# Hybrid SSD/attention layer on one core: transposed products as three 256-column matmuls per contraction tile, weights shifted by 64 bytes

## The chip, the cores and the metric

The kernel runs on one core of a Trainium2 chip. The metric is the device time of one execution in microseconds (us); lower is better. TensorE (PE) multiplies; its weight loads (PEld) are instructions of their own. ScalarE (ACT) and VectorE (DVE) do the elementwise work, GpSimd (POOL) a little of it, and SyncE (SP) issues most DMAs.

## The reference

One layer for 256 tokens of width 2048, all in float32:

```python
h = rmsnorm(x, g_mix) @ w_in                 # 2048 -> 5728 columns
z, xbc, dt, q, k, v, qi, ki, wi = _split(h, IN_SIZES)
xbc = jax.nn.silu(causal_dwconv(xbc, conv_w, conv_b))
...                                          # y_ssd: chunked SSD, gated by z, normalized
...                                          # y_att: attention over 64 keys chosen by the qi, ki, wi scores
x = x + jnp.concatenate([y_ssd, y_att], axis=-1) @ w_out      # 2048 -> 2048
u = rmsnorm(x, g_mlp) @ w_up                                  # 2048 -> 8192
return x + jnp.square(jax.nn.relu(u)) @ w_down                # 8192 -> 2048
```

The four weight matrices hold 207 MB less a little, and each is read from HBM once.

## The kernel before

**Split operands.** Every operand of a big product is split into two float32r parts, hi (the rounded value) and lo (the rest), and a product is the sum of three partial products: hi·hi, lo·hi and hi·lo. `operands` (L110) makes the parts of a weight block: SP loads `raw`, ACT casts it to `whi` (L122), DVE subtracts to get `wlo` (L123). `raw` has RB = 4 buffers, `whi` and `wlo` WB = 5 each. All this is emitted with a priority 600 instructions ahead of its place (HP); ACT and DVE are ordered by a scheduler that goes by such priorities, TensorE by the program's order alone (`manual_schedule`).

**Two kinds of product.** In `product` the tokens stand on the output's partitions: the activations are the stationary operand (the "weights" of TensorE) and the weight block streams as the moving operand, three matmuls of 512 columns (304 in the blocks m0 and m1) per token block and contraction tile, L141 to L143. In `product_t` the output's columns stand on partitions: 128-column slices of `whi` and `wlo` are the stationary operand, and the activations stream. The activations stand in `hx` or `x2x`, for each contraction tile `kt` as 512 columns, hi of the 256 tokens and then lo. L181 streams all 512 over the hi weights, into both halves of an accumulator bank (hi·hi in the first half, lo·hi in the second), L182 streams the first 256 over the lo weights into the second half. `total` adds the halves (L190, L191). One call of `product_t` makes 32 such pairs: four `operands` blocks of 1024 columns, eight slices each.

**Where `product_t` stands.** In the input projection for the blocks qi (4 calls) and xbc (6 calls), with `hx` streaming, and in the MLP for `w_up` (32 calls), with `x2x` streaming: 42 calls, 1344 pairs. The MLP runs up(0), up(1), down(0), up(2), down(1), up(3), down(2), down(3), where down is `product` on `w_down`. Between the big products the tasks of a list (SSD, attention, top-k choice) are advanced by `step`, a few instructions of PE at a time. The block m1, a `product` with 304 columns, follows the ten calls of the input projection; at that time DVE also does the convolution (L497) and the top-k choice (L469, L470).

**Addresses.** The tiles are allocated one behind the other in each partition, so their addresses follow from their sizes. In the built program `hx` (and `x2x`, in the same place) begins at byte 17632, the `whi` buffers at 87264 and every 4096 bytes on, the `wlo` buffers at 107744 and every 4096 on, `uh` and `ul` (the activations of down) at 129504 and further. All of these are 96 more than a multiple of 128. Two unused tiles, `gap0` (192 bytes, ahead of `hx`) and `gap1` (64 bytes, behind it), are part of that arrangement. In the blocks m0 and m1 alone, every second contraction tile streams from the second half of a block of 608 columns, 1216 bytes further on, which is 64 more than a multiple of 128, while its stationary operand stays where it was.

Of the kernel before, what the change touches and what calls it, by code (L numbers as in the profile page):

```python
# [10 lines left out]
F32R = mybir.dt.float32r  # L11
# [5 lines left out]
P = 128  # L17
D = 2048
T = 256
NB = T // P  # L20
KT = D // P
# [7 lines left out]
WARM = 9  # L29
WB = 5  # L30
RB = 4


Z0, XBC0, DT0, Q0, K0, V0, QI0, KI0, WI0, END = (
# [31 lines left out]
def hymba_kernel(ctx: ExitStack, tc: tile.TileContext, xn, xt, w_in, w_out, w_up, w_down, vcol, vrow, out):  # L66
    nc = tc.nc
    ctx.enter_context(tc.manual_schedule(engines={nc.tensor.engine}))
    keep = ctx.enter_context(tc.tile_pool(name="keep", bufs=1))
    wts = ctx.enter_context(tc.tile_pool(name="wts", bufs=1))  # L70
# [24 lines left out]
    def step():  # L95
        for t in list(tasks):
            if isinstance(t[1], int) and t[1] > 0:
                t[1] -= 1
            elif not isinstance(t[1], str) or t[1] in done:
                advance(t)  # L100
# [6 lines left out]
        return vc[:, VC[name] + i:VC[name] + i + 1]  # L107


    def operands(src, n, load=None):  # L110

        with tc.high_priority(offset=HP):
            raw = wts.tile([P, n], F32, name="raw", tag="raw", bufs=RB)
            hi = wts.tile([P, n], F32R, name="whi", tag="whi", bufs=WB)
            lo = wts.tile([P, n], F32R, name="wlo", tag="wlo", bufs=WB)
            step = n if load is None else n // 2
            for i in range(0, n, step):
                s = slice(i, i + step)
                nc.sync.dma_start(raw[:, s], src[:, s])
                if load is not None:  # L120
                    load()
                nc.scalar.copy(hi[:, s], raw[:, s])  # L122
                nc.vector.tensor_tensor(lo[:, s], raw[:, s], hi[:, s].bitcast(F32), op=OP.subtract)  # L123
        return hi, lo
# [4 lines left out]
    def accumulators():  # L129
        return [ps.tile([P, 512], F32, name="acc", tag="acc") for _ in range(2)]  # L130

    def product(src, n, left, load=None, tail=None):
# [16 lines left out]
        for kt in range(KT):  # L149
            if kt % 2 == 0:  # L150
                hi, lo = operands(src[kt // 2], 2 * n, load)
            w = slice(kt % 2 * n, kt % 2 * n + n)
            wh, wl = hi[:, w], lo[:, w]
            if kt < last:
                part(kt, acc[0][:, :n], 0, wh, wl)
                if tail is None:
                    part(kt, acc[1][:, :n], 1, wh, wl)
                else:
                    for i, (b, c) in enumerate(halves):
                        part(kt, acc[1 + i][:, c], b, wh[:, c], wl[:, c])  # L160
            else:
                kept.append((kt, wh, wl))
            step()
# [7 lines left out]
    def product_t(src, right):  # L171

        acc = accumulators()
        for i in range(4):
            hi, lo = operands(src[i], 1024)
            c = i % 2
            for k in range(8):
                kt = 8 * (i // 2) + k
                x = right(kt)
                s = slice(k * P, (k + 1) * P)  # L180
                nc.tensor.matmul(acc[c], hi[:, s], x, start=(kt == 0), stop=False)  # L181
                nc.tensor.matmul(acc[c][:, T:], lo[:, s], x[:, :T], start=False, stop=(kt == KT - 1))  # L182
                if k % 4 == 3:
                    step()
        return acc
# [53 lines left out]
    for name, cols in IN_BLOCKS:  # L239
        n = sum(b - a for a, b in cols)  # L240
# [8 lines left out]
    def in_pair(name, i):  # L249
        o = in_off[name][0] + i * 256 * D  # L250
        return product_t(w_in[o:o + 256 * D].rearrange("(h p c) -> h p c", h=4, p=P), lambda kt: hx[:, kt, :])
# [501 lines left out]
    def x2(kt):  # L753
        if kt >= KT - 4:
            need("res3")
        return box[0][:, kt, :]

    first = product_t(w_up[0], x2)
    while tasks:
        step()  # L760
# [11 lines left out]
    def up(q):  # L772
        uh = mlp.tile([P, KT, T], F32R, name="uh")
        ul = mlp.tile([P, KT, T], F32R, name="ul")
        for j in range(8):
            r = mlp.tile([P, 2, T], F32, name="r")
            total(r, first if q + j == 0 else product_t(w_up[8 * q + j], x2))
            nc.vector.scalar_tensor_tensor(r, r, 0.0, r, op0=OP.max, op1=OP.mult)
            s = slice(2 * j, 2 * j + 2)
            nc.scalar.copy(uh[:, s, :], r)  # L780
            nc.vector.tensor_tensor(ul[:, s, :], r, uh[:, s, :].bitcast(F32), op=OP.subtract)
        return uh, ul
# [72 lines left out]
```

## Time and profile before

| | |
|---|---|
| time before, median of 3 runs | 1114.1 us (1113.76 to 1115.49) |
| the profiled execution: its time | 1113.72 us |
| its span in the trace | 1111.7 us |
| PE busy | 1101.4 us, 99% of the span |
| PEld busy | 938.4 us, 84% |
| DVE busy | 692.5 us, 62% |
| ACT busy | 534.2 us, 48% |
| HBM read | 204.29 MB, 186 GB/s over the span with what is written |

The span is the time from the first to the last instruction in the trace. Matmuls are pipelined, and a row's own duration contains its latency; what a stream of them costs is read from the spacing of their starts in the timeline. Times in the trace are counted from the start of the span.

### The profile page before, as it was taken

Reading aid. Unit: us, or ns where it says so; the run is one execution under the profiler, and the core shown is the slowest. Engines: PE = TensorE matmul, PEld = TensorE weight load, DVE = VectorE, ACT = ScalarE, POOL = GpSimd, SP = SyncE. Lnnn points to the kernel's source line nnn. Section 1 sums busy time; section 2 is a strip of 40 time slices with the busy share of each in tenths; the row PEclk is TensorE's granted clock in tenths of the full one; section 3 lists DMA queues with packets and bytes.
Section 4 is the critical chain, followed back from the end, with each engine's and each line's share of the span. In section 5 each row is a group of like instructions: output and inputs, shape, how many; then the busy total and the mean of one; then the engine's idle time right before and its main releaser. Section 6 shows DMA issues by size and latency. Waiting matters only on the chain.

```text
span 1111.7 us, 14959 instructions
## 1 busy us (share of the span) xinstructions
PE 1101.4 (99%) x5686; PEld 938.4 (84%) x5686; DVE 692.5 (62%) x976; ACT 534.2 (48%) x749; POOL 41.5 (4%) x41
## 2 busy tenths in 40 slices
PE   9999998999999999999999999999999999999998
PEld 7888887888888888888888888888888888888887
DVE  6786989677765565656564455565555565555443
ACT  7755655556755444444444334444334444333341
POOL 0010131112000000000000000000000000000000
PEclk9999999999999999999999999999999999999999
DMA  9855435644376555556555665556666556666662
GB/s 309 276 191 186 155 106 167 197 152 133 118 261 187 176 187 187 184 182 188 188 189 190 193 196 183 188 188 191 193 195 193 181 186 190 196 194 194 209 212 73
DMA packets 63735, 207.36 MB, mean 187 GB/s; under 512 B 7216, under 2 KB 11568, under 8 KB 63664
## 3 DMA queue, kind: packets, MB, share of 16 engines
q1 hardware_dynamic: 63520, 206.36, 58.0%
q8 instruction: 45, 0.74, 0.3%
q14 instruction: 26, 0.21, 0.0%
q10 hardware_dynamic: 144, 0.05, 0.0%
HBM read 204.29 MB, written 2.10 MB: 186 GB/s over the span
## 4 chain that ended last, share of the span: by engine, by line
PE 95%; DVE 3%; issue 1%; DMA 0%; ACT 0%; POOL 0%; DVEq 0%; POOLq 0%; ACTq 0%
PE acc L181 27%; PE acc L141 17%; PE acc L143 16%; PE acc L142 16%; PE acc L182 14%; DVE wlo L123 1%; DVE bc L497 1%; PE ps_y L568 1%; DVE sc L461 1%; PE ps_sr L652 0%; PE ps_l L606 0%; PE ps_o L631 0%; DMA raw<-in_w_in 0%; PE ps_w L200 0%; PE ps_dec L559 0%
## 5 line engine op out<-in xcount | busy, mean ns | idle before, releaser
L123 DVE TENSOR_TENSOR wlo<-raw,whi 128x1024 fp32r<-128x1024 f32 (+3 forms) x400 | 467.0, 1170 | 382.9 <-ACT whi L122 380.0
L122 ACT CAST whi<-raw 128x1024 fp32r<-128x1024 f32 (+3 forms) x400 | 400.0, 1003 | 500.0 <-PE acc L142 247.0
L181 PE MATMUL acc<-x2x,whi 128*128 128x512 f32 x1024 | 362.2, 399 | 0.0
L182 PE MATMUL acc<-x2x,wlo 128*128 128x256 f32 x1024 | 287.6, 281 | 0.0
L181 PEld LDWEIGHTS acc<-x2x,whi 128*128 128x128 f32 x1024 | 192.4, 188 | 47.8
L142 PE MATMUL acc<-whi,ul 128*128 128x512 f32 (+1 forms) x512 | 197.6, 386 | 0.0
L141 PE MATMUL acc<-whi,uh 128*128 128x512 f32 (+1 forms) x512 | 197.6, 386 | 0.0
L143 PE MATMUL acc<-wlo,uh 128*128 128x512 f32 (+1 forms) x512 | 197.5, 386 | 0.0
L182 PEld LDWEIGHTS acc<-x2x,wlo 128*128 128x128 f32 x1024 | 193.4, 189 | 0.1
L181 PE MATMUL acc<-hx,whi 128*128 128x512 f32 x320 | 113.9, 398 | 0.0
L141 PEld LDWEIGHTS acc<-whi,uh 128*128 128x128 f32 x512 | 96.1, 188 | 19.6
L143 PEld LDWEIGHTS acc<-wlo,uh 128*128 128x128 f32 x512 | 96.1, 188 | 19.4
L142 PEld LDWEIGHTS acc<-whi,ul 128*128 128x128 f32 x512 | 96.2, 188 | 19.3
L182 PE MATMUL acc<-hx,wlo 128*128 128x256 f32 x320 | 89.7, 280 | 0.0
L143 PE MATMUL acc<-wlo,hx 128*128 128x512 f32 (+1 forms) x224 | 82.7, 369 | 3.3 <-DVE wlo L123 3.1
L141 PE MATMUL acc<-whi,hx 128*128 128x512 f32 (+1 forms) x224 | 85.4, 381 | 0.0
L142 PE MATMUL acc<-whi,hx 128*128 128x512 f32 (+1 forms) x224 | 82.1, 367 | 0.0
L181 PEld LDWEIGHTS acc<-hx,whi 128*128 128x128 f32 x320 | 60.2, 188 | 13.6
L182 PEld LDWEIGHTS acc<-hx,wlo 128*128 128x128 f32 x320 | 60.5, 189 | 0.0
L143 PEld LDWEIGHTS acc<-wlo,hx 128*128 128x128 f32 x224 | 42.3, 189 | 11.7 <-DVE wlo L123 5.2
L141 PEld LDWEIGHTS acc<-whi,hx 128*128 128x128 f32 x224 | 42.4, 189 | 6.9 <-issue 0.7
L142 PEld LDWEIGHTS acc<-whi,hx 128*128 128x128 f32 x224 | 42.4, 189 | 6.5 <-issue 0.7
(224 smaller groups left out, 828.9 us busy)
## 6 DMA issues: line engine op xcount, KB each, us to landing
raw<-in_w_up SPq DMA_DIRECT2D x128, 512.0 KB, 3.6
raw<-in_w_down SPq DMA_DIRECT2D x128, 512.0 KB, 4.2
raw<-in_w_in SPq DMA_DIRECT2D x72, 512.0 KB, 3.7
raw<-in_w_out SPq DMA_DIRECT2D x32, 512.0 KB, 3.6
raw<-in_w_in SPq DMA_DIRECT2D x16, 256.0 KB, 4.4
raw<-in_w_in SPq DMA_DIRECT2D x16, 152.0 KB, 5.3
raw<-in_w_in SPq DMA_DIRECT2D x8, 304.0 KB, 2.8
xT<-in_xt SPq DMA_DIRECT2D x16, 128.0 KB, 4.3
```

The costliest lines, as they stand in the source:

```text
L122: nc.scalar.copy(hi[:, s], raw[:, s])
L123: nc.vector.tensor_tensor(lo[:, s], raw[:, s], hi[:, s].bitcast(F32), op=OP.subtract)
L141: nc.tensor.matmul(out, ah[:, s], wh, start=(kt == 0), stop=False)
L142: nc.tensor.matmul(out, al[:, s], wh, start=False, stop=False)
L143: nc.tensor.matmul(out, ah[:, s], wl, start=False, stop=(kt == KT - 1))
L181: nc.tensor.matmul(acc[c], hi[:, s], x, start=(kt == 0), stop=False)
L182: nc.tensor.matmul(acc[c][:, T:], lo[:, s], x[:, :T], start=False, stop=(kt == KT - 1))
L461: nc.vector.scalar_tensor_tensor(sc[:, :nk], rl[:, i, :nk], wis[:, b, h:h + 1], neg[:, T - nk:] if first else sc[:, :nk], op0=OP.mult, op1 ...
L497: nc.vector.scalar_tensor_tensor(o[:, j, :], pad[:, j, k:k + T], vcp("conv_w", 12 * k + ct), o[:, j, :], op0=OP.mult, op1=OP.add)
L568: nc.tensor.matmul(pt[:, 64 * i:64 * i + 64], m[i // 4][:, i % 4, :], xdt[:, c, 64 * h:64 * h + 64], start=True, stop=True)
```

## The change

`operands` allocates one tile for both parts, of 2n columns and 64 spare ones, and takes hi and lo as slices of it that begin `shift` elements in. `product` uses shift 0, `product_t` 16 elements, 64 bytes. The L181 matmul of 512 columns becomes two of 256, and the order in a contraction tile is hi weights on hi activations, lo weights on hi activations, hi weights on lo activations. Each has a weight load of its own, so the hi slice is loaded twice.

```diff
+SPARE = 64
+SHIFT_T = 16
...
-    def operands(src, n, load=None):
+    def operands(src, n, load=None, shift=0):
...
-            hi = wts.tile([P, n], F32R, name="whi", tag="whi", bufs=WB)
-            lo = wts.tile([P, n], F32R, name="wlo", tag="wlo", bufs=WB)
+            both = wts.tile([P, 2 * n + SPARE], F32R, name="w2", tag="w2", bufs=WB)
+            hi, lo = both[:, shift:shift + n], both[:, shift + n:shift + 2 * n]
...
-            hi, lo = operands(src[i], 1024)
+            hi, lo = operands(src[i], 1024, shift=SHIFT_T)
...
-                nc.tensor.matmul(acc[c], hi[:, s], x, start=(kt == 0), stop=False)
-                nc.tensor.matmul(acc[c][:, T:], lo[:, s], x[:, :T], start=False, stop=(kt == KT - 1))
+                nc.tensor.matmul(acc[c][:, :T], hi[:, s], x[:, :T], start=(kt == 0), stop=False, skip_group_check=True)
+                nc.tensor.matmul(acc[c][:, T:], lo[:, s], x[:, :T], start=False, stop=False, skip_group_check=True)
+                nc.tensor.matmul(acc[c][:, T:], hi[:, s], x[:, T:], start=False, stop=(kt == KT - 1),
+                                 skip_group_check=True)
```

In the built program of the change the joint buffers begin at byte 87264 and every 8448 bytes on, so hi and lo stand 96 behind a multiple of 128 in `product`, as before, and 32 behind one in `product_t`; `hx` and `x2x` keep their place, and all tiles behind the buffers move by 1280 bytes.

On TensorE the place is the inside of `product_t` in the MLP. Before, with `whi` and `wlo` as the weights and `x2x` streaming:

```order
L181 MATMUL acc<-x2x,whi 128x512
L182 MATMUL acc<-x2x,wlo 128x256
L181 MATMUL acc<-x2x,whi 128x512
L182 MATMUL acc<-x2x,wlo 128x256
L181 MATMUL acc<-x2x,whi 128x512
L182 MATMUL acc<-x2x,wlo 128x256
```

Now, where `w_4162` is one joint buffer and lines are 3 to 5 higher:

```order
L184 MATMUL acc<-x2x,w_4162 128x256
L185 MATMUL acc<-x2x,w_4162 128x256
L186 MATMUL acc<-x2x,w_4162 128x256
L184 MATMUL acc<-x2x,w_4162 128x256
L185 MATMUL acc<-x2x,w_4162 128x256
L186 MATMUL acc<-x2x,w_4162 128x256
L184 MATMUL acc<-x2x,w_4162 128x256
L185 MATMUL acc<-x2x,w_4162 128x256
L186 MATMUL acc<-x2x,w_4162 128x256
```

A contraction tile has three rows in the place of two, and each row has 256 columns. The order around `product_t` is the same on TensorE.

The scheduler also orders DVE's queue anew around the end of the input projection. The place is that of the weight blocks of m1 (608 columns each): before, with `sc` the scores from which the top-k choice takes its maxima and `bc` the convolution's output,

```order
L123 TENSOR_TENSOR wlo<-raw,whi 128x608
L191 TENSOR_TENSOR xraw<-acc,xraw 128x256
L469 MAX m_2011<-sc_1689 128x8
L470 MATCH_REPLACE sc_1689<-m_2011,sc_1689 128x256
L123 TENSOR_TENSOR wlo<-raw,whi 128x608
L497 SCALAR_TENSOR_TENSOR bc<-pad,vc,bc 128x256 x3
L123 TENSOR_TENSOR wlo<-raw,whi 128x608
L497 SCALAR_TENSOR_TENSOR bc<-pad,vc,bc 128x256 x2
L123 TENSOR_TENSOR wlo<-raw,whi 128x608
```

and now

```order
L126 TENSOR_TENSOR w_2302<-raw,w_2302 128x608
L196 TENSOR_TENSOR xraw<-acc,xraw 128x256
L475 MATCH_REPLACE sc_1907<-m_2272,sc_1907 128x256
L474 MAX m_2292<-sc_1907 128x8
L126 TENSOR_TENSOR w_2322<-raw,w_2322 128x608
L502 SCALAR_TENSOR_TENSOR bc<-pad,vc,bc 128x256 x2
L126 TENSOR_TENSOR w_2342<-raw,w_2342 128x608
L502 SCALAR_TENSOR_TENSOR bc<-pad,vc,bc 128x256 x3
L126 TENSOR_TENSOR w_2374<-raw,w_2374 128x608
```

Between the last four of m1's subtractions stand the same kinds of instructions in nearly the same number; one convolution step stands one subtraction later, and the search and replace steps of the choice have traded places.

## Rows read from the trace of the kernel before

**Rows 1.** Page, busy time of the engines and the granted TensorE clock in 40 slices

```profile
PE 1101.4 (99%) x5686; PEld 938.4 (84%) x5686; DVE 692.5 (62%) x976; ACT 534.2 (48%) x749; POOL 41.5 (4%) x41
...
PEclk9999999999999999999999999999999999999999
```

**Rows 2.** Page, the chain that ended last, shares by engine and by line

```profile
PE 95%; DVE 3%; issue 1%; DMA 0%; ACT 0%; POOL 0%; DVEq 0%; POOLq 0%; ACTq 0%
PE acc L181 27%; PE acc L141 17%; PE acc L143 16%; PE acc L142 16%; PE acc L182 14%; DVE wlo L123 1%; DVE bc L497 1%; PE ps_y L568 1%; DVE sc L461 1%; PE ps_sr L652 0%; PE ps_l L606 0%; PE ps_o L631 0%; DMA raw<-in_w_in 0%; PE ps_w L200 0%; PE ps_dec L559 0%
```

**Rows 3.** Page, groups: busy us, mean ns of one, idle before and what ended it

```profile
L122 ACT CAST whi<-raw 128x1024 fp32r<-128x1024 f32 (+3 forms) x400 | 400.0, 1003 | 500.0 <-PE acc L142 247.0
L181 PE MATMUL acc<-x2x,whi 128*128 128x512 f32 x1024 | 362.2, 399 | 0.0
L182 PE MATMUL acc<-x2x,wlo 128*128 128x256 f32 x1024 | 287.6, 281 | 0.0
L181 PE MATMUL acc<-hx,whi 128*128 128x512 f32 x320 | 113.9, 398 | 0.0
```

**Rows 4.** Timeline of PE inside w_up: start us, duration us, instruction

```profile
699.89 0.40 PE L181 MATMUL acc<-x2x,whi 128*128 128x512 f32 x1
700.13 0.28 PE L182 MATMUL acc<-x2x,wlo 128*128 128x256 f32 x1
700.25 0.40 PE L181 MATMUL acc<-x2x,whi 128*128 128x512 f32 x1
...
700.95 0.40 PE L181 MATMUL acc<-x2x,whi 128*128 128x512 f32 x1
```

**Rows 5.** Windows (length; PE, PEld, DVE, ACT, POOL busy us): qi/xbc, m1, up(0, 1), up(2)

```profile
100.00:168.00 68.00, 68.00 (x416) 60.46 (x415) 58.83 (x112) 38.50 (x67) 14.45 (x13) 1.00 0.43 136
168.00:188.00 20.00, 16.30 (x109) 14.87 (x108) 19.55 (x40) 10.57 (x18) 4.08 (x3) 1.00 0.47 140
396.40:578.20 181.80, 181.80 (x1034) 157.87 (x1033) 113.05 (x147) 86.26 (x118) 0.00 (x0) 1.00 0.59 186
665.30:755.70 90.40, 90.40 (x513) 78.44 (x512) 54.21 (x63) 41.23 (x54) 0.00 (x0) 1.00 0.59 187
```

**Rows 6.** Waits of PE over the span: us in total, times, longest

```profile
PE acc L143 <- DVE wlo L123: 3.1, 3, 1.8
```

**Rows 7.** Timeline of PE inside down(0): only 512-column matmuls

```profile
600.00 0.39 PE L141 MATMUL acc<-whi,uh 128*128 128x512 f32 x1
...
600.68 0.39 PE L141 MATMUL acc<-whi,uh 128*128 128x512 f32 x1
```

**Rows 8.** Timeline of PE at the end of down(3): only 256-column matmuls

```profile
1105.90 0.28 PE L141 MATMUL acc<-whi,uh 128*128 128x256 f32 x1
1106.02 0.28 PE L142 MATMUL acc<-whi,ul 128*128 128x256 f32 x1
1106.14 0.28 PE L143 MATMUL acc<-wlo,uh 128*128 128x256 f32 x1
...
1107.34 0.28 PE L141 MATMUL acc_t<-whi,uh 128*128 128x256 f32 x1
```

**Rows 9.** Timeline of PE, plain float32 matmuls of 64 and 256 columns, merged to their end

```profile
220.56 1.61 PE L568 MATMUL ps_y<-room,mt 128*128 128x64 f32 x13
...
221.23 0.94 PE L568 MATMUL ps_y<-room,mt 128*128 128x64 f32 x7
...
239.21 1.46 PE L606 MATMUL ps_l<-room,qT 128*128 128x256 f32 x6
...
239.86 0.81 PE L606 MATMUL ps_l<-room,qT 128*128 128x256 f32 x3
```

**Rows 10.** Timeline of PE inside m1: first matmul of contraction tiles 0 to 4

```profile
168.10 0.30 PE L141 MATMUL acc<-whi,hx 128*128 128x304 f32 x1
...
168.93 0.30 PE L141 MATMUL acc<-whi,hx 128*128 128x304 f32 x1
...
169.76 0.30 PE L141 MATMUL acc<-whi,hx 128*128 128x304 f32 x1
...
170.59 0.30 PE L141 MATMUL acc<-whi,hx 128*128 128x304 f32 x1
...
171.43 0.30 PE L141 MATMUL acc<-whi,hx 128*128 128x304 f32 x1
```

## Prediction

> **What bounds the kernel now.** I read the page's busy times first: TensorE is busy 99% of the span, and its granted clock is full in every slice, that is 2.4 GHz [rows 1]. The chain of waits says the same from the other end: 95% of what ended last is TensorE, and 41% of it are the two lines that the change touches, L181 and L182 [rows 2]. So a nanosecond on each of their matmuls is a nanosecond on the kernel, but the groups can't give that price: one L181 is listed with 399 ns and one L182 with 281 [rows 3], and these overlap. The price is the spacing of starts. Inside w_up three pairs take from 699.89 to 700.95 us, 1060 ns, so a pair costs 353.3 ns [rows 4]. That the pair is repeated 1024 + 320 = 1344 times is in the groups' counts [rows 3]; 1344 x 353.3 ns = 475 us, which is the 41 to 43% of the chain. In the windows of up(0) to up(2) TensorE has no idle time at all, while DVE is busy for 60% and ACT for less than half [rows 5]: there nothing but TensorE's own stream sets the pace. The one wait of note is in m1, where TensorE waits 3.1 us for DVE's subtraction [rows 6], and DVE is busy for 19.55 of 20 us [rows 5].
>
> **What a matmul of each size costs.** Where 512-column matmuls follow one another, three take 600.00 to 600.68, 226.7 ns each [rows 7]. 512 columns at 2.4 GHz are 213.3 ns, so 13.3 ns are lost on each. Where only 256-column matmuls follow one another, each with a weight load of its own, twelve take 1105.90 to 1107.34: 120.0 ns each [rows 8], again 13.3 over their 106.7. The loss is one for each matmul, whatever its length. The mixed pair loses 33.3 over the 320 ns of its 768 columns, a little more than twice 13.3; the split of this is not to be seen.
>
> **The change, part by part.**
>
> *Three matmuls of 256.* The columns stay 768. By the row that is nearest, the 256-column stream [rows 8], a contraction tile costs 3 x 120.0 = 360.0 ns in the place of 353.3: +6.7 ns, x 1344 = **+9.0 us**, of which 6.8 in the MLP (1024) and 2.1 in qi and xbc (320). The third weight load is in the 120 ns: each matmul of that row loads its own. The bounds: below, if each of the three lost as little as the L182 of a pair seems to, 0.12 us from 700.13 to 700.25 at this row's resolution [rows 4], nothing would be lost or gained; at the very least a weight load needs some spacing, and the tightest stream of loads and matmuls in the trace, 64-column ones at full latency, has (221.23 - 220.56)/6 = 112 ns [rows 9]; 3 x 112 = 336 would be -17.3 ns, -23.3 us. Above, another loss of the same size, 13.3 ns per matmul, would be +62.7 us.
>
> The Trainium skill (TensorE: Matmul & The Clock Gate, Back-to-back issue gap) gives a warm matmul N/2.4 + 2.5 ns. By that the triple would cost one 2.5 ns more than the pair, an estimate of +3.4 us; the rows show a loss of 13.3, not 2.5, for float32r matmuls that each load weights, so the measurement decides, and the sign is the same.
>
> *64 bytes.* This is the part that the trace nearly lacks. Everywhere else stationary and moving operand begin at the same place modulo 128 bytes. The exception is m1: in its odd contraction tiles the weights begin 64 bytes further, modulo 128, than what streams, just as in the change. Tiles 0 and 2 (even) take 168.10 to 168.93 and 169.76 to 170.59, 0.83 us each for six matmuls; tiles 1 and 3 (odd) 0.83 and 0.84 [rows 10]. So 138.3 to 140 ns for 304 columns, 11.7 to 13.3 over their 126.7 in both positions. I take the shift at nothing. It has a doubt: six matmuls and then the other position, so the row does not show a long stream in the shifted one. Taking the low end of it, 11.7, the triple is 355.0, +1.7 ns, +2.3 us.
>
> What speaks for an effect is that the 13.3 ns are not the price of exchanging weights: plain float32 matmuls of 256 columns, a load each, are spaced (239.86 - 239.21)/3 = 217 ns [rows 9], about 3 over two passes of 106.7. They ask for their moving columns at half the pace. So the loss looks like two readers in each other's way, and that could depend on the address.
>
> The Trainium skill speaks against it (TensorE: Matmul & The Clock Gate, What happens when you issue a matmul): streaming and loading have independent read ports, and loading the next weights takes no read bandwidth from the running matmul. By that the shift is worth exactly nothing; no row here shows the ports themselves.
>
> *Joint buffers.* A cast into a joint buffer now has to wait until the last reader of either part is done, one matmul later at most (0.23 us). ACT is idle for 500 us ahead of its casts, 247 of them waiting for TensorE to free a buffer [rows 3], because it runs up to five blocks ahead; that lead covers it, and I cost it at nothing. In m1, where there is no lead, it could cost 8 blocks x 0.14 = 1.1 us.
>
> *DVE's new order.* The rows from the built programs show the same work between m1's last subtractions, a convolution step later by one. TensorE reaches m1 2.1 us later, for DVE partly time won: of the 3.1 us of waiting [rows 6] I give back one. The bound is 2.1 back or 2 more.
>
> *Sum*, against the profiled execution's own 1113.72 us: +6.8 + 2.1 - 1.0 = +7.9, 1121.6. The median of the runs is 0.4 us higher, so for the measurement **1122.0 us**, +0.7%. Its own range is 1116.4 (11.7 ns lost per matmul) to 1125 (all of the 9.0 and 2 us more waiting in m1).
>
> **The rivals.**
>
> 1. *Faster: the 64 bytes part the two readers.* Then the loss per matmul falls from 13.3 towards 5, the 112 ns of the tightest row [rows 9]: -23.3 us, 1090.8. Half of the loss gone (113.3 ns, 340 per tile) gives -17.9, 1096. It decides from 117.8 ns on: below that the triple is cheaper than the pair. For it: the float32 rows, whose loss is small though weights change as often. Against: the odd tiles of m1, which show nothing of it. The forecast of this case is 1093, and its range 1090 to 1111.
>
> 2. *No change.* The stream of three keeps the L182's 117 to 118 ns [rows 4] in place of the 120 of the pure stream, and 3 x 117.8 is the pair's 353.3. That gives 1114, and with what m1 does 1112 to 1116.
>
> 3. *Much slower: the shifted stream falls in a worse beat.* One half of the loss more on each matmul, 126.7 ns, is 380 per tile: +26.7 ns, +35.8 us, 1150. For it only that the mixed pair already loses more than its parts do; against it again m1.
>
> **How the numbers follow.** A difference of 0.2% (2.2 us) is about what measuring this kernel can tell from none. The forecast has 0.45, since its price comes from a stream of the same matmuls and the one shifted row agrees; the faster rival 0.39, because the shifted position in a long stream is nowhere in the trace and the loss that it could remove is as large as 13.3 x 3 per tile; no change 0.09; much slower 0.07. So faster 0.39, within 0.2% 0.09, slower 0.52. The range has to take in the faster rival: 1090 to 1125 leaves out the much slower case and a few hundredths below the tightest row, under 2 in 10; the forecast alone is 1116.4 to 1125.
>
> **What would show it.** In the timeline of w_up, three starts of L184 to L186 every 360 ns and 0.12 us between any two; windows of up(2) and up(3) of 92.1 us in place of 90.4 [rows 5] with no idle TensorE; the products of w_down and w_out unchanged at 226.7 ns; the wait for DVE in m1 between 1 and 5 us; ACT and DVE no nearer to being the bound. The prediction is wrong if the spacing is not near 120 in the shifted stream: at 112 to 117 the first rival holds, above 122 the third. If the spacing is 120 and the time is not 1120 to 1124, the step on m1 and DVE's order is the wrong one.

## The result and the profile after

The changed kernel takes 1107.24 us (median, 1105.94 to 1107.8) against 1113.93 us: a ratio of 0.9938, 95% interval 0.9921 to 0.9955. It is 0.6% faster; 1122.0, slower, was forecast. 1107 lies in the stated range, in the faster rival.

The page's busy times and chain answer to [rows 1, 2]: the bound has not moved, TensorE is still 99% busy, and the touched lines L184 to L186 still hold 41% of the chain.

```profile
span 1105.5 us, 17621 instructions
...
PE 1095.9 (99%) x7030; PEld 995.0 (90%) x7030; DVE 693.0 (63%) x976; ACT 534.6 (48%) x749; POOL 42.5 (4%) x41
...
PE acc L146 16%; PE acc L144 16%; PE acc L145 16%; PE acc L186 14%; PE acc L185 14%; PE acc L184 13%; DMA raw<-in_w_in 1%; DVE w L126 1%; PE ps_y L573 1%; DMA xrow<-in_xn 1%; PE ps_sr L657 0%; PE ps_l L611 0%; PE ps_o L636 0%; DMA xT<-in_xt
```

Where the time came from is read by stage. The windows of the changed kernel are cut where the first matmul of a stage starts: qi and xbc, m1, up(0) and up(1), up(2), up(3). Columns as in [rows 5].

```profile
42.50:166.70 124.20, 123.17 (x1060) 122.53 (x1059) 106.67 (x216) 71.36 (x119) 20.54 (x17) 1.00 0.53 171
166.70:188.20 21.50, 18.11 (x109) 17.24 (x108) 20.51 (x41) 9.76 (x17) 4.15 (x3) 0.84 0.47 133
396.80:571.90 175.10, 175.10 (x1545) 175.09 (x1544) 112.98 (x147) 86.40 (x118) 0.00 (x0) 1.00 0.60 193
659.00:749.40 90.40, 90.40 (x769) 90.39 (x768) 54.28 (x63) 41.28 (x54) 0.00 (x0) 1.00 0.58 187
836.50:926.90 90.40, 90.40 (x769) 90.37 (x768) 54.27 (x63) 41.28 (x54) 0.00 (x0) 1.00 0.57 187
```

The same cuts before, for the first two and the last stage:

```profile
42.30:168.10 125.80, 124.14 (x739) 109.26 (x739) 104.51 (x216) 71.14 (x119) 20.06 (x17) 1.00 0.52 169
168.10:187.80 19.70, 16.00 (x109) 14.61 (x108) 19.25 (x40) 10.57 (x18) 3.98 (x3) 1.00 0.47 141
...
842.80:933.20 90.40, 90.40 (x513) 78.35 (x512) 54.23 (x63) 41.25 (x54) 0.00 (x0) 1.00 0.59 187
```

qi and xbc gained 1.6 us and m1 gave back 1.8. up(0) and up(1) gained 181.8 - 175.1 = 6.7 us [rows 5]. up(2) and up(3), the same code, gained nothing. The sum, -6.5, is the span's 1111.7 to 1105.5 but for 0.3.

The timeline says what differs. One matmul in w_up, L184, ten triples apart, in up(1) and in up(2):

```profile
499.86 0.28 PE L184 MATMUL acc<-x2x,w 128*128 128x256 f32 x1
...
503.26 0.28 PE L184 MATMUL acc<-x2x,w 128*128 128x256 f32 x1
...
700.00 0.28 PE L184 MATMUL acc<-x2x,w 128*128 128x256 f32 x1
...
703.53 0.28 PE L184 MATMUL acc<-x2x,w 128*128 128x256 f32 x1
```

340 ns a triple in up(1), 113.3 a matmul; 353 in up(2), 117.7. Both are under the 120.0 of [rows 8] on which the forecast stood, and the second is what the old pair cost [rows 4]. Each holds for a whole stage, so these are two settled beats (steady spacings of the starts), not scatter. qi and xbc, where other tasks cut the stream into stretches of some 4 to 60 triples, have both: each stretch keeps 340 or 353 ns from its third triple to its end.

The place where one changes into the other is in up(0), at transposes of another task (L657):

```profile
401.13 0.28 PE L184 MATMUL acc<-x2x,w 128*128 128x256 f32 x1
401.25 0.28 PE L185 MATMUL acc<-x2x,w 128*128 128x256 f32 x1
401.37 0.28 PE L186 MATMUL acc<-x2x,w 128*128 128x256 f32 x1
401.49 0.60 PE L657 MATMUL ps_sr<-ident,xr 128*128 128x128 f32 x4
401.85 0.37 PE L184 MATMUL acc<-x2x,w 128*128 128x256 f32 x1
...
402.51 0.28 PE L186 MATMUL acc<-x2x,w 128*128 128x256 f32 x1
402.62 0.28 PE L184 MATMUL acc<-x2x,w 128*128 128x256 f32 x1
402.74 0.28 PE L185 MATMUL acc<-x2x,w 128*128 128x256 f32 x1
402.85 0.28 PE L186 MATMUL acc<-x2x,w 128*128 128x256 f32 x1
```

Ahead of them the starts are 0.12 us apart, some matmuls behind them 0.11, and so it stays to the end of up(1).

### The profile page after: what moved, and what is told of

It reads as the page before. It is cut to its first block, busy times and chain, and to the rows that moved or that the text cites. A ratio compares the mean times of both kernels' runs of the same rounds, so it can differ in the third digit from the quotient of the medians.

```text
span 1105.5 us, 17621 instructions
## 1 busy us (share of the span) xinstructions
PE 1095.9 (99%) x7030; PEld 995.0 (90%) x7030; DVE 693.0 (63%) x976; ACT 534.6 (48%) x749; POOL 42.5 (4%) x41
## 4 chain that ended last, share of the span: by engine, by line
PE 93%; DVE 3%; DMA 2%; ACT 1%; issue 1%; SPq 0%; ACTq 0%; DVEq 0%
PE acc L146 16%; PE acc L144 16%; PE acc L145 16%; PE acc L186 14%; PE acc L185 14%; PE acc L184 13%; DMA raw<-in_w_in 1%; DVE w L126 1%; PE ps_y L573 1%; DMA xrow<-in_xn 1%; PE ps_sr L657 0%; PE ps_l L611 0%; PE ps_o L636 0%; DMA xT<-in_xt 0%; PE ps_s L459 0%
## 5 line engine op out<-in xcount | busy, mean ns | idle before, releaser
L126 DVE TENSOR_TENSOR w<-raw,w 128x1024 fp32r<-128x1024 f32 (+3 forms) x400 | 468.4, 1174 | 379.4 <-ACT w L125 378.5
L125 ACT CAST w<-raw 128x1024 fp32r<-128x1024 f32 (+3 forms) x400 | 399.8, 1002 | 491.1 <-PE acc L146 255.4
L184 PE MATMUL acc<-x2x,w 128*128 128x256 f32 x1024 | 285.4, 279 | 0.0
L185 PE MATMUL acc<-x2x,w 128*128 128x256 f32 x1024 | 285.2, 279 | 0.0
L186 PE MATMUL acc<-x2x,w 128*128 128x256 f32 x1024 | 285.2, 279 | 0.0
L145 PE MATMUL acc<-w,ul 128*128 128x512 f32 (+1 forms) x512 | 197.6, 386 | 0.0
L144 PE MATMUL acc<-w,uh 128*128 128x512 f32 (+1 forms) x512 | 197.5, 386 | 0.0
L146 PE MATMUL acc<-w,uh 128*128 128x512 f32 (+1 forms) x512 | 197.5, 386 | 0.0
L185 PEld LDWEIGHTS acc<-x2x,w 128*128 128x128 f32 x1024 | 194.4, 190 | 0.1
L184 PEld LDWEIGHTS acc<-x2x,w 128*128 128x128 f32 x1024 | 192.2, 188 | 0.1
L186 PEld LDWEIGHTS acc<-x2x,w 128*128 128x128 f32 x1024 | 192.2, 188 | 0.0
L144 PEld LDWEIGHTS acc<-w,uh 128*128 128x128 f32 x512 | 96.1, 188 | 19.4
L146 PEld LDWEIGHTS acc<-w,uh 128*128 128x128 f32 x512 | 96.1, 188 | 19.4
L184 PE MATMUL acc<-hx,w 128*128 128x256 f32 x320 | 89.9, 281 | 0.0
L185 PE MATMUL acc<-hx,w 128*128 128x256 f32 x320 | 89.2, 279 | 0.0
L186 PE MATMUL acc<-hx,w 128*128 128x256 f32 x320 | 89.2, 279 | 0.0
L146 PE MATMUL acc<-w,hx 128*128 128x512 f32 (+1 forms) x224 | 83.7, 373 | 3.5 <-DVE w L126 3.3
L144 PE MATMUL acc<-w,hx 128*128 128x512 f32 (+1 forms) x224 | 86.4, 386 | 0.3 <-ACT w L125 0.3
L145 PE MATMUL acc<-w,hx 128*128 128x512 f32 (+1 forms) x224 | 83.2, 371 | 0.0
L184 PEld LDWEIGHTS acc<-hx,w 128*128 128x128 f32 x320 | 60.6, 189 | 0.0
L186 PEld LDWEIGHTS acc<-hx,w 128*128 128x128 f32 x320 | 60.3, 188 | 0.0
```

The costliest lines, as they stand in the source:

```text
L144: nc.tensor.matmul(out, ah[:, s], wh, start=(kt == 0), stop=False)
L145: nc.tensor.matmul(out, al[:, s], wh, start=False, stop=False)
L146: nc.tensor.matmul(out, ah[:, s], wl, start=False, stop=(kt == KT - 1))
L184: nc.tensor.matmul(acc[c][:, :T], hi[:, s], x[:, :T], start=(kt == 0), stop=False, skip_group_check=True)
L186: nc.tensor.matmul(acc[c][:, T:], hi[:, s], x[:, T:], start=False, stop=(kt == KT - 1), skip_group_check=True)
```

## The experiments

Two questions: which part of the change makes the spacing shorter, and why half of w_up gains nothing. The kernels are the change with one thing altered, if not said otherwise. Each is set against runs of the kernel before on the same chip; a kernel with a single time has no ratio.

**Three matmuls, no shift.**

```diff
-SHIFT_T = 16
+SHIFT_T = 0
```

> The change with the shift at 0: joint buffers and three matmuls of 256, the weights at the same place modulo 128 bytes as what streams. Theory S (the 64 bytes make the shorter spacing): every triple of w_up takes 360.0 ns, 120.0 a matmul, in all four up stages, and the time is 9 us over before, 1121 to 1124. Theory T (three equal matmuls in this order make it, wherever the weights lie): 340 or 353.3 ns as in the change, 1105 to 1108. If S holds, the step of the prediction on three matmuls was right and the one on the 64 bytes was wrong.

Measured: 1122.84 us against 1113.87, ratio 1.0085 (1.007 to 1.01). Ten triples:

```profile
699.73 0.28 PE L184 MATMUL acc<-x2x,w 128*128 128x256 f32 x1
...
703.33 0.28 PE L184 MATMUL acc<-x2x,w 128*128 128x256 f32 x1
```

360 ns each. Theory S holds: without the 64 bytes the change is the forecast's, +9.0 us where +9.0 was the term. Three equal matmuls as such lose.

**The shift, with the old pair.**

```diff
-                nc.tensor.matmul(acc[c][:, :T], hi[:, s], x[:, :T], start=(kt == 0), stop=False, skip_group_check=True)
-                nc.tensor.matmul(acc[c][:, T:], lo[:, s], x[:, :T], start=False, stop=False, skip_group_check=True)
-                nc.tensor.matmul(acc[c][:, T:], hi[:, s], x[:, T:], start=False, stop=(kt == KT - 1),
-                                 skip_group_check=True)
+                nc.tensor.matmul(acc[c], hi[:, s], x, start=(kt == 0), stop=False)
+                nc.tensor.matmul(acc[c][:, T:], lo[:, s], x[:, :T], start=False, stop=(kt == KT - 1))
```

> Joint buffers and the shift of 64 bytes with the old pair of a 512- and a 256-column matmul. Theory S with one loss for each weight load: the loss per matmul falls from 13.3 to between 6.7 and 11 as in the change, so the pair of 353.3 falls to between 333 and 342 ns, and the time to 1090 to 1100, below the change. Theory T: the pair stays at 353.3 ns and the time at 1113 to 1115.

Measured: 1115.26 us against 1113.87, ratio 1.0019 (1.0008 to 1.003). Ten pairs:

```profile
699.72 0.40 PE L184 MATMUL acc<-x2x,w 128*128 128x512 f32 x1
...
703.25 0.40 PE L184 MATMUL acc<-x2x,w 128*128 128x512 f32 x1
```

353 ns, as before. The expectation from theory S was wrong: the shift alone gains nothing with a 512- and a 256-column matmul. It needs the three equal ones; neither part gains by itself.

**Joint buffers alone**: the pair as above, and SHIFT_T = 0.

> Joint buffers alone: shift 0 and the old pair. Theories S and T both: no effect, pairs of 353.3 ns, 1112.5 to 1115.5. Theory J (that both parts lie in one buffer, and all that is behind it moves, is what helps): 1105 to 1110.

Measured: 1115.02 us, ratio 1.0006 (0.9997 to 1.0016): no change that can be told in the whole. Where the parts lie, and that all tiles behind them move, gains nothing; m1 alone is longer here, which the next section takes up.

**128, 32 and 192 bytes.**

```diff
-SHIFT_T = 16
+SHIFT_T = 32    # and 8, and 48
```

> Three matmuls with the weights 128 bytes further. If what counts is the place modulo 128 bytes, this is as shift 0: 360.0 ns a triple, 1121 to 1124. If it is modulo 256, or any distance helps: 340 to 353.3 ns, 1100 to 1109. Theory T: 1105 to 1108.

> Three matmuls with the weights 32 bytes further. If the place modulo 64 bytes or the exact 64 counts, the triple is 360 ns or worse and the time 1120 to 1130. If any place but the same one helps, 340 to 353 ns and 1100 to 1109.

> Three matmuls with the weights 192 bytes further. If the place modulo 128 bytes decides, it is as 64: triples of 340.0 and 353.3 ns, one time of 1103 to 1108. If 64 bytes more, not less, is what helps: 360 ns, 1120 to 1124.

Measured: 128 bytes 1120.39 us (ratio 1.0061, 1.0046 to 1.0076); 32 bytes 1116.39 (1.0021, 1.0012 to 1.0031); 192 bytes, one time only, 1114.09. Ten triples at about 700 us, with 128, 32 and 192 bytes:

```profile
699.82 0.28 PE L184 MATMUL acc<-x2x,w 128*128 128x256 f32 x1
...
703.42 0.28 PE L184 MATMUL acc<-x2x,w 128*128 128x256 f32 x1
```

```profile
699.74 0.28 PE L184 MATMUL acc<-x2x,w 128*128 128x256 f32 x1
...
703.29 0.28 PE L184 MATMUL acc<-x2x,w 128*128 128x256 f32 x1
```

```profile
699.91 0.28 PE L184 MATMUL acc<-x2x,w 128*128 128x256 f32 x1
...
703.44 0.28 PE L184 MATMUL acc<-x2x,w 128*128 128x256 f32 x1
```

360, 355 and 353 ns. With 192 bytes there is the slower beat of the change in all of w_up; the one time, 1114, is that of pairs of the same length. The faster beat is there too, in stretches of qi and xbc, where ten triples take 3.40 us:

```profile
111.89 0.28 PE L184 MATMUL acc<-hx,w 128*128 128x256 f32 x1
...
115.29 0.28 PE L184 MATMUL acc<-hx,w 128*128 128x256 f32 x1
```

So 192 bytes have the same two beats as 64, and differ in which stretch gets which. With 128 bytes up(2) runs as with 0. But up(0) and up(1) do not:

```profile
499.89 0.28 PE L184 MATMUL acc<-x2x,w 128*128 128x256 f32 x1
...
503.45 0.28 PE L184 MATMUL acc<-x2x,w 128*128 128x256 f32 x1
```

That is 356 ns at 128 bytes, which no stage of w_up at shift 0 has. The place modulo 128 bytes alone would then not decide, unless 0 has this beat too and neither kernel with shift 0 fell into it. The expectations for 32 and 192 missed: 32 bytes gave neither 360 nor a gain, and 192 gave the spacings of 64 but not its time.

**The shift in the other products too**, where the joint buffer streams and `uh`, `ul` are the weights.

```diff
-                hi, lo = operands(src[kt // 2], 2 * n, load)
+                hi, lo = operands(src[kt // 2], 2 * n, load, shift=SHIFT_T)
```

> The change, and the shift of 64 bytes in the other kind of product too, where the joint buffer is what streams: 2016 matmuls of 512 columns now start 64 bytes further than their weights. Theory D (any stream of equal matmuls loses less when the two places differ by 64 bytes): 512-column matmuls fall from 226.7 to 220 ns, 13 us less, 1093 to 1096. Theory P (it depends on the pair of lengths, and 512 has its beat already): 226.7 ns as before and 1106 to 1109. A worse beat, 233 ns, would give 1120.

Measured: 1111.15 us against 1113.47, ratio 0.9974 (0.9964 to 0.9984), slower than the change. Thirty 512-column matmuls in down(0), and then ten triples in up(1) and in up(2):

```profile
599.76 0.40 PE L144 MATMUL acc<-w,uh 128*128 128x512 f32 x1
...
606.76 0.40 PE L144 MATMUL acc<-w,uh 128*128 128x512 f32 x1
...
499.97 0.28 PE L184 MATMUL acc<-x2x,w 128*128 128x256 f32 x1
...
503.50 0.28 PE L184 MATMUL acc<-x2x,w 128*128 128x256 f32 x1
...
699.98 0.28 PE L184 MATMUL acc<-x2x,w 128*128 128x256 f32 x1
...
703.38 0.28 PE L184 MATMUL acc<-x2x,w 128*128 128x256 f32 x1
```

In down(0) 512 columns take 233 ns, against 226.7 with both at the same place [rows 7]. Elsewhere in this kernel they take 229, in down(1) to down(3) and in the 512-column products of w_out and w_in. Thirty in down(1), and then twelve 256-column matmuls at the end of down(3):

```profile
780.13 0.39 PE L144 MATMUL acc<-w,uh 128*128 128x512 f32 x1
...
787.00 0.39 PE L144 MATMUL acc<-w,uh 128*128 128x512 f32 x1
...
1102.64 0.28 PE L144 MATMUL acc<-w,uh 128*128 128x256 f32 x1
...
1104.00 0.28 PE L144 MATMUL acc_t<-w,uh 128*128 128x256 f32 x1
```

So 512 columns have two beats at 64 bytes as well, and both are slower than the one at 0: theory D is out. The slowest one, 233 in all of them, would have given the 1120 of the expectation (the trace has 2352 such matmuls, not 2016). The twelve of 256 columns take 1.36 us, 113.3 ns each. This is the end of down(3) from which the forecast took its 120.0 [rows 8], and here it is the moving operand that lies 64 bytes further. The two beats in w_up have changed sides: up(1) runs at 353 and up(2) at 340 ns a triple, with nothing altered in w_up itself. What comes ahead of it was altered.

**Choosing the beat.** Some transposes of the unit matrix, read by nothing, ahead of two stages:

```diff
+    def relock(n):
+        pt = ps.tile([P, 512], F32, name="ps_k", tag="mid")
+        for i in range(n):
+            nc.tensor.transpose(pt[:, i * P:(i + 1) * P], ident, ident)
+
     def up(q):
+        if q > 1:
+            relock(4 if q == 2 else 2)
```

> The change with a few plain float32 transposes of the unit matrix, whose result nothing reads, ahead of up(2) (four) and up(3) (two). In the change these two stages run with 353.3 ns a triple throughout, up(0) and up(1) with 340.0 from the second group of transposes of another task on. Theory L (two beats, and what comes ahead of a stream chooses): with luck one or both stages change to 340.0 ns, 3.4 us less for each, less 0.5 for the transposes: 1101 to 1105. Theory M (up(2) and up(3) are slower for another reason, such as where u lies or what DVE and ACT do): both stay at 353.3 and the time rises by 0.8 us, 1107 to 1109.

Measured: 1100.08 us against 1113.47, ratio 0.9875 (0.9856 to 0.9895), 6 to 7 us below the change. The windows of up(2) and up(3) in this kernel, and ten triples of up(2):

```profile
657.40:744.90 87.50, 87.50 (x773) 87.46 (x772) 54.09 (x63) 41.27 (x55) 0.00 (x0) 1.00 0.60 193
831.80:919.30 87.50, 87.50 (x773) 87.46 (x771) 54.26 (x63) 41.44 (x55) 0.00 (x0) 1.00 0.60 193
```

```profile
700.03 0.28 PE L184 MATMUL acc<-x2x,w 128*128 128x256 f32 x1
...
703.43 0.28 PE L184 MATMUL acc<-x2x,w 128*128 128x256 f32 x1
```

Both stages changed to 340 ns. Theory L holds: u's place was the same, and DVE and ACT were busy for the same 54 and 41 us. The times of this kernel lie within 1.8 us, those of the change within 1.9; one stage in the other beat would be 3 us more or less, so by the times the choice repeats from one execution to the next. Two controls tell whether the transposes gain by themselves: the kernel before with the same `relock`, and three matmuls at shift 0 with it.

> The kernel before with the same transposes ahead of up(2) (four) and up(3) (two). The trace of before has pairs of 346.67 ns in some stretches of qi and xbc and 353.33 in all of w_up. If the transposes gain by themselves, whatever the shift, pairs in up(2) and up(3) fall to 346.67 ns, 3.4 us less, less 0.8 for the transposes: 1110.5 to 1112.5. If they only choose between the two beats that the shift makes, 353.3 ns stay and the time is 1114 to 1116.

> Three matmuls with shift 0 and the same transposes. If the second beat of 340.0 ns is owed to the 64 bytes, all of w_up stays at 360.0 ns a triple and the one time is 1122 to 1125. If transposes alone choose the beat, up(2) and up(3) fall below 360 ns and the time below 1119.

Measured: before with `relock` 1113.71 us, ratio 1.0001 (0.9991 to 1.001); shift 0 with it, one time only, 1124.56. Ten pairs and ten triples of them:

```profile
699.80 0.40 PE L181 MATMUL acc<-x2x,whi 128*128 128x512 f32 x1
...
703.34 0.40 PE L181 MATMUL acc<-x2x,whi 128*128 128x512 f32 x1
```

```profile
699.80 0.28 PE L184 MATMUL acc<-x2x,w 128*128 128x256 f32 x1
...
703.40 0.28 PE L184 MATMUL acc<-x2x,w 128*128 128x256 f32 x1
```

354 and 360 ns, as without transposes. They choose between beats; the one of 340 is seen with a shift of 64 or 192 bytes alone.

## Why the prediction was wrong

**The step that failed** is the one on the 64 bytes: "I take the shift at nothing." The shift changes what a triple costs from 360 to 340 or 353 ns: -20.0 or -6.7 ns, not 0. With the counts of w_up alone, half at either, that is 512 x 20.0 + 512 x 6.7 = 13.7 us, the bulk of the 15.6 us between the kernel without the shift (1122.84) and the change (1107.24).

The row on which that step stood was read rightly and carried too far. In m1's odd tiles [rows 10] the weights do begin 64 bytes further than what streams, but for six matmuls and of 304 columns. The experiments show that the length may not be left out: the shift gains nothing for the mixed pair and harms 512 columns. That the row was short is not shown to be the reason, for twelve matmuls of 256 columns already had 113.3 ns; a long shifted stream of 304 columns was not tried. The doubt was written beside it; it should have weighed more than the row.

**Three matmuls of 256** was right to the tenth: +9.0 forecast, 1122.84 - 1113.87 = 9.0 with shift 0. By that kernel's windows w_up became 6.8 us longer and qi and xbc 2.3, against terms of 6.8 and 2.1, and up(2) took the 92.1 us that the prediction named; that the whole fits as closely is in part luck, since m1 was 0.9 longer and what stands ahead of qi 0.9 shorter. The 120.0 ns of [rows 8] carried over. The bound, the chain and the count were right as well.

**The rule on the read ports** (the Trainium skill, TensorE: Matmul & The Clock Gate, What happens when you issue a matmul) would have made kernels that differ in the weights' address alone the same. They run at 120.0, 118.3 and 113.3 ns a matmul; the measurements decide, and loading weights is not independent of the running matmul's reads here, or something else in the address counts. The N/2.4 + 2.5 ns of the Trainium skill (TensorE: Matmul & The Clock Gate, Back-to-back issue gap), by an estimate 109.2 for 256 columns, was reached in no run: the shortest spacing was 113.3.

**Joint buffers at nothing** was right for the whole time (ratio 1.0006), but not for m1.

**DVE's order and m1** had the wrong sign: 1.0 us was to come back, and m1 became 1.8 us longer. TensorE reached it 1.4 us earlier, but that does not explain it. With three matmuls and no shift TensorE reached m1 1.4 us later than before, and m1 was still 0.9 us longer; with joint buffers alone it was 1.3 longer:

```profile
169.50:190.10 20.60, 15.88 (x108) 14.68 (x107) 19.61 (x41) 9.66 (x17) 3.56 (x3) 1.00 0.43 134
167.10:188.10 21.00, 16.07 (x108) 14.72 (x107) 20.19 (x41) 9.75 (x17) 3.89 (x3) 1.00 0.44 133
```

TensorE's longest wait for DVE in m1 is 1.8 us before [rows 6], 2.7 in the change, 2.5 and 2.7 in these two. What the three share is the joint buffers and the order that DVE's queue got with them; no run separates these. The prediction had bounds of 2 us for DVE's order and 1.1 us for the joint buffers in m1, and the 1.8 lie within them. In the change's m1 the granted clock fell to 1.2 GHz for a part, 0.84 over the stage, behind TensorE's wait of 2.7 us; this is not the cause either, for the kernel with `relock` had 1.00 there and its m1 took 21.15 us.

**The first rival** had the mechanism's place and its point of decision, 117.8 ns a matmul, and the change has one beat on that very point and one under it. Its 1096 for 113.3 ns took the fast one for all; the version with `relock`, which has it in nearly all of w_up, comes to about 4 us above that. That the loss fell by half was one of its own cases; why it fell is not shown. The rival of no change has its 117.8 ns in up(2) and up(3), but not its time, and the much slower rival is out.

**What stays open:** why an address 64 bytes further helps. That two readers meet in the memory is argued from the float32 rows [rows 9] and from the address mattering at all; no run shows the meeting itself. `hx` and `x2x` were never moved, so it is also not shown whether the distance counts or the weights' own place; the end of down(3) with the moving operand shifted speaks for the distance. Nor is it known what in the transposes moves a stream from one beat to the other: in up(0) of the change the first group of four did not and the second did, with the shift in all products the same groups moved up(0) from 340 to 353 ns, and with 192 bytes they left it at 353.

## What to carry to other kernels

A stream of matmuls that load weights each can settle in one of several beats, so time it in every stage where it stands, in the very lengths and places that the kernel will use; a row with another length does not price it, and a single stretch shows one beat of several. Where a stage of the same code runs at two spacings in one trace, look at what precedes it: a few small instructions ahead of it can be worth 3% of the stage. Where two edits are made together, one may be worth something only with the other, so undo each by itself before either is credited.

## What was not expected of the hardware

- The spacing of 256-column float32r matmuls depends on how much further one operand begins than the other: 120.0 ns at 0 bytes, 118.3 at 32, 113.3 or 117.7 at 64 and at 192, 118.7 or 120.0 at 128.
- The best distance depends on the length: 512 columns take 226.7 ns at 0, and 233 (down(0)) or 229 (everywhere else) at 64.
- At 64 bytes there are two settled beats for the same instructions, and two plain float32 transposes ahead of a stage of 768 matmuls were enough to get the shorter one for all of it. Other groups of transposes led to the longer one.
- The kernel before had two beats as well, unseen when the forecast was made: ten pairs of qi took 46.77 to 50.24 us, 347 ns each, in place of 353.3.

```profile
46.77 0.39 PE L181 MATMUL acc<-hx,whi 128*128 128x512 f32 x1
...
50.24 0.39 PE L181 MATMUL acc<-hx,whi 128*128 128x512 f32 x1
```
